# Issuing the first of two stores from ScalarE's queue instead of SyncE's in a row-normalising kernel

## The chip, the cores and the metric

The kernel runs on one core of one Trainium2 chip. The metric is the device time of one execution in microseconds (us), as the median of several runs; lower is better. The profile's span, from first to last instruction, is some 1.8 us shorter than the time of the same execution.

## The reference

Each of 1024 rows of 4096 floats is divided by its Euclidean norm.

```python
x = np.random.randn(1024, 4096).astype(np.float32)      # eps = 1e-12
norm = np.sqrt(np.sum(x ** 2, axis=-1, keepdims=True) + eps)
out = (x / norm).astype(np.float32)
```

## The kernel before

The rows lie in two groups. A group is one tile of 128 partitions with 4 rows each (8.39 MB), loaded by one transfer and stored by one. Both loads are issued at the start by SyncE. Per group, VectorE squares and sums row 3, ScalarE rows 0 to 2, and VectorE scales the rows. Only row 2 of the first group is scaled by both engines, ScalarE taking 7/8 of it.

```python
    for i in range(n_tiles):                       # n_tiles = 2
        g = RowGroups(...)
        load = nc.sync.dma_start(out=g.flat(), in_=x_t[i])
        if i == 0:
            first_load_to_front(nc, load.ins)      # ahead of the start-up barrier
        groups.append(g)

    for i, g in enumerate(groups):
        g.square_dve(R - 1)
        g.square_act(0)
        # ... cut: norm and scale of rows 0, 1 and 3 ...
        g.square_act(2)
        g.norm(2)
        if i < n_tiles - 1:
            g.scale_by_both(2)                     # ScalarE 3584 columns, VectorE 512
        else:
            g.scale(2)                             # VectorE alone
        store = nc.sync.dma_start(out=out_t[i], in_=g.flat())
    gpsimd_waits_for_last_store(nc, store.ins)     # shortens the end; not touched
```

## Time and profile before

| What | Value |
|---|---|
| Time, median of 6 runs | 81.93 us (81.73 to 81.96) |
| Span of the profiled run (82.04 us, 0.1 above the six) | 80.2 us |
| First store issued / second store issued | 38.99 / 56.76 us |
| Second load landed | 41.37 us |
| Last landing | 80.03 us |

The prediction shows the views that bound the kernel. Below, an *engine* without a name is one of the 16 DMA engines, and the *ring* of a queue is its part on one such engine. Each engine moves a transfer as eight data packets of 65,536 bytes and a last packet of 4 bytes, the *completion*; the transfer has landed when all 16 completions have arrived. In a table of windows, each line gives the window, its width, the busy times of the engines, the clock, the share of the 16 DMA engines, and GB/s. A data packet is booked whole in the window in which it starts. So when a window holds exactly one data packet of each engine, *share times width* is the mean time of that packet, and GB/s times width is 16 x 65,536 bytes = 1.05 MB. These are the first packets of the first store in the kernel before:

```profile
40.26:41.06 0.80, 0.00 (x0) 0.00 (x0) 0.00 (x0) 1.00 3.05 1311
41.06:42.88 1.82, 1.48 (x1) 1.48 (x1) 0.00 (x0) 1.00 0.00 0
42.88:43.48 0.60, 0.60 (x1) 0.60 (x1) 0.00 (x0) 1.00 4.03 1748
```

1311 GB/s x 0.80 us = 1.05 MB, so this is one packet of each engine, and 3.05 x 0.80 = 2.44 us is its mean time. The second packets (4.03 x 0.60 = 2.42 us) start from 42.88 on.

### The profile page before, as it was taken

The page shows a single profiled execution, that of the slowest core. Times are in us where ns is not written, and L with a number is a line of the kernel's source. Part 1 is how long each engine was busy: PE and PEld are TensorE (multiplying, and loading weights), DVE is VectorE, ACT ScalarE, POOL GpSimd, SP SyncE. Part 2 cuts the span into 40 slices and gives each one's busy share as a digit, 9 for nine tenths or more (in the row PEclk, how much of TensorE's full clock was granted, in tenths as well). Part 3 has the DMA queues.
Part 4 walks back from the last instruction along what each step waited for, and adds up shares of the span by engine and source line. Part 5 has one row for each costly group of instructions (what it writes and reads, how often), then busy time and mean ns, then how long its engine had stood idle before and what let it go on. Part 6 is the DMA issues. An engine that isn't in the chain of part 4 may idle for free.

```text
span 80.2 us, 93 instructions
## 1 busy us (share of the span) xinstructions
DVE 26.7 (33%) x21; ACT 29.7 (37%) x23; POOL 0.2 (0%) x4
## 2 busy tenths in 40 slices
DVE  0000000000099599960039995999200000000000
ACT  6000000000099999989439999950000000000000
POOL 0000000000000000000000000000000000000000
DMA  9099996699996699996699990999991999992990
GB/s 490 33 523 523 523 490 294 261 523 523 523 490 261 294 523 523 523 490 261 294 523 523 523 490 33 523 523 523 523 458 65 523 523 523 523 425 98 523 523 0
DMA packets 576, 33.55 MB, mean 418 GB/s; under 512 B 64, under 2 KB 64, under 8 KB 64
## 3 DMA queue, kind: packets, MB, share of 16 engines
q1 hardware_dynamic: 576, 33.55, 97.4%
HBM read 16.78 MB, written 16.78 MB: 418 GB/s over the span
## 4 chain that ended last, share of the span: by engine, by line
DMA 51%; ACT 10%; DVE 9%; issue 0%
DMA xt<-in_x_dram 51%; ACT sq_act L33 9%; DVE xt L64 9%; ACT rstd L53 1%; DVE rstd L59 0%
## 5 line engine op out<-in xcount | busy, mean ns | idle before, releaser
L33 ACT ACTIVATE sq_act<-xt 128x4096 f32<-128x4096 f32 x6 | 21.7, 3609 | 22.4 <-DMA xt<-in_x_dram 22.4
L42 DVE SCALAR_TENSOR_TENSOR sq_dve<-xt 128x4096 f32<-128x4096 f32 x2 | 8.9, 4426 | 26.4 <-DMA xt<-in_x_dram 26.4
L64 DVE TENSOR_SCALAR xt<-xt,rstd 128x4096 f32<-128x4096 f32 x7 | 16.5, 2353 | 0.2
L72 ACT ACTIVATE xt<-xt,rstd 128x3584 f32<-128x3584 f32 x1 | 3.3, 3283 | 0.2 <-DVE rstd L59 0.2
L53 ACT ACTIVATE rstd<-ssq,eps_t 128x1 f32<-128x1 f32 x8 | 2.1, 290 | 0.1
L59 DVE RECIPROCAL rstd<-rstd 128x1 f32<-128x1 f32 x8 | 1.3, 160 | 2.5 <-ACT rstd L53 2.5
L33 ACT ACT_TABLE_LOAD x1 | 1.3, 1283 | 0.8 <-PEq L258 0.8
L53 ACT ACT_TABLE_LOAD x1 | 1.3, 1283 | 0.0
L33 ACT ACTIVATION_READ_ACCUMULATOR sq_act<-xt 128x1 f32 x6 | 1.1, 187 | 0.0
L78 DVE TENSOR_SCALAR xt<-xt,rstd 128x512 f32<-128x512 f32 x1 | 0.5, 487 | 0.0
L211 DVE MEMSET eps_t<- 128x1 f32 x1 | 0.1, 59 | 0.9 <-PEq L258 0.9
L42 DVE DVE_READ_ACCUMULATOR sq_dve<-xt 128x1 f32 x2 | 0.2, 83 | 0.0
L258 POOL MEMSET const-uint8-127<- 128x1 uint8 x1 | 0.1, 103 | 0.0
L258 POOL MEMSET const-bfloat16-1.0<- 128x1 bf16 x1 | 0.1, 102 | 0.0
L258 POOL MEMSET const-float32-0.0<- 128x1 f32 x1 | 0.1, 99 | 0.2 <-issue 0.2
L258 POOL MEMSET const-float32-1.0<- 128x1 f32 x1 | 0.1, 99 | 0.0
## 6 DMA issues: line engine op xcount, KB each, us to landing
xt<-in_x_dram SPq DMA_DIRECT2D x2, 31.3
out_dram<-xt SPq DMA_DIRECT2D x2, 22.5
```

Of the source, the lines that this page charges most:

```text
L33: self.nc.scalar.activation(out=sq_a, in_=self.x[:, r], func=ACT_F.Square, accum_out=self.ssq[:, r : r + 1],)
L42: self.nc.vector.scalar_tensor_tensor(out=sq_v, in0=self.x[:, r], scalar=1.0, in1=self.x[:, r], op0=ALU.mult, op1=ALU.mult, accum_out=self ...
L53: self.nc.scalar.activation(out=self.rstd[:, r : r + n], in_=self.ssq[:, r : r + n], func=ACT_F.Sqrt, bias=self.eps_t,)
L59: self.nc.vector.reciprocal(out=self.rstd[:, r : r + n], in_=self.rstd[:, r : r + n])
L64: self.nc.vector.tensor_scalar_mul(out=self.x[:, r], in0=self.x[:, r], scalar1=self.rstd[:, r : r + 1])
L72: self.nc.scalar.activation(out=self.x[:, r, :cut], in_=self.x[:, r, :cut], func=ACT_F.Copy, scale=rstd,)
L78: self.nc.vector.tensor_scalar_mul(out=self.x[:, r, cut:], in0=self.x[:, r, cut:], scalar1=rstd)
L211: nc.vector.memset(eps_t, eps)
L258: nc = _bacc.Bacc("TRN2", target_bir_lowering=False, num_devices=1)
```

## The change

The first store moves to ScalarE's queue, behind the shared scale that ScalarE computes itself. SyncE then need not wait for another engine's result before this store, and the store does not lie in the same queue as the load before it.

```diff
-        store = nc.sync.dma_start(out=out_t[i], in_=g.flat())
+        queue = nc.scalar if i < n_tiles - 1 else nc.sync
+        store = queue.dma_start(out=out_t[i], in_=g.flat())
```

The scheduler also reorders ScalarE's instructions in the second group: the square root of row 3 comes first there, as in the first group.

## The prediction

> **What bounds the kernel now.** I read the page first, then the chain that ended last, then the waits of the DMA-issuing engine, then the timeline and the packet starts around the one moment that the change touches. The page's queue part comes first, because it says at once what can be won:
>
> ```profile
> span 80.2 us, 93 instructions
> DVE 26.7 (33%) x21; ACT 29.7 (37%) x23; POOL 0.2 (0%) x4
> q1 hardware_dynamic: 576, 33.55, 97.4%
> HBM read 16.78 MB, written 16.78 MB: 418 GB/s over the span
> ```
>
> No engine is busy for even half of the span, while the packets of the single queue fill 97.4% of what 16 DMA engines have: 78.1 of 80.2 us. The 16.78 MB in and 16.78 MB out are compulsory. The packet records show how they move: each engine carries 32 packets of 65,536 bytes, nearly all of 2.418 us, one straight after another, so 16 x 65,536 / 2.418 us = 434 GB/s while they flow, and 32 x 2.418 = 77.4 us is a floor under the span. The other 2.8 us are the 1.0 to 2.1 us before the first packets start and some 0.3 us between the last packet and its landing, with a few tenths in between. So the kernel is bound by the transfers, and no order of issue can win more than tenths.
>
> The chain of waits shows two places where compute stands between the transfers:
>
> ```profile
> 0.79 40.58 DMA xt<-in_x_dram
> 41.40 3.72 ACT sq_act L33 x2
> 54.38 2.35 DVE xt L64
> ```
>
> The second load lands at about 41.4; the second group's compute then runs to 56.73, and only then can the second store be issued. That chain ends long before the span does, because the second store then lies in the queue behind the first. The waits of the DMA-issuing engine and the timeline give the moments:
>
> ```profile
> SPq L240 <- DVE xt L64: 15.3, 1, 15.3
> SPq L240 <- ACT xt L72: 2.8, 1, 2.8
> ...
> 35.68 3.28 ACT L72 ACTIVATE xt<-xt,rstd 128x3584 f32<-128x3584 f32 x1 [0.23 <-DVE rstd L59]
> 38.99 18.11 SPq L240 DMA_DIRECT2D out_dram<-xt  x2
> 41.40 3.62 ACT L33 ACTIVATE sq_act<-xt 128x4096 f32<-128x4096 f32 x1 [2.43 <-DMA xt<-in_x_dram]
> ```
>
> The shared scale on ScalarE ends at 38.97, the first store is issued at 38.99, with no delay that the change could take away. ScalarE then idles for 2.43 us for the second load. What the engines do there, by the starts of their packets:
>
> ```profile
> 37.80:38.70 0.90, 0.00 (x0) 0.90 (x1) 0.00 (x0) 1.00 2.70 1165
> 38.70:40.26 1.56, 0.00 (x0) 0.27 (x1) 0.00 (x0) 1.00 0.00 0
> 40.26:40.47 0.21, 0.00 (x0) 0.00 (x0) 0.00 (x0) 1.00 0.01 0
> 40.47:41.06 0.59, 0.00 (x0) 0.00 (x0) 0.00 (x0) 1.00 4.13 1777
> ```
>
> The last load packets start by 38.7. Then nothing starts until 40.26, where the first of the load's 4-byte completion packets are (share 0.01, 0 GB/s). From 40.47 to 41.06 the store's first 16 packets start (1777 GB/s x 0.59 us = 1.05 MB). Packet by packet, the load's last data packets end between 40.265 and 41.053 on the 16 engines, a completion packet follows each at once, and on eleven engines a store packet 5 to 6 ns after that. On the other five the load ended at 40.27 to 40.49 and the store started only at 40.49 to 40.68. Those five tell the latency of the store: 1.50 to 1.69 us from issue to its first packets.
>
> **What the Trainium skill says.** "DMA: Bandwidth & Descriptors", section "Issuing engines are not separate DMA queues": transfers from ScalarE and SyncE run on the same 16 DMA engines and interleave; a second issuer saves only the issue time. The trace agrees as far as it can: the 434 GB/s above is the "Fabric ceiling" of 435 GB/s that the same page's "Specifications" give, so a second queue has no bandwidth to find. The same page, "Queues, rings and completion order": SP and ACT each have a ring of their own on each of the 16 engines, and an engine takes turns between its rings "at *packet* granularity"; the completion increment lands only after every earlier write of that engine, across its queues. The trace of before has one queue in this stretch, so it shows neither; it shows the opposite order, where the load's completion always goes ahead of the store's data.
>
> **The change part by part.** Removed: SyncE's issue of the first store (348 ns on an engine that then waits anyway): 0. Added: the same issue on ScalarE, some 0.35 us out of the 2.43 us for which it waits: 0. Its conditions are the same last instructions (the shared scale on both engines), so the issue stays at about 39.0.
>
> Moved by the scheduler: the order listing shows ScalarE's instructions of the second group in another order. The square root of the row that VectorE squared now goes first and waits for it; the order becomes that of the first group. Cost, counted from the landing: before, the last scale ends at 54.38 + 2.35 - 41.40 = 15.33 us. After, the first root starts when VectorE's accumulator is read, 45.75 + 0.08 - 41.40 + 0.04 = 4.47 us; in the first group the last scale starts 35.68 - 27.11 = 8.57 us after the first root, and takes 2.35: 15.39 us. So ScalarE's later second square (about 0.9 us) is paid back by VectorE having a second row to scale meanwhile, and the net is about +0.05 us, off the path.
>
> What matters is the ring. With its own ring the store does not have to queue behind the load's completion packet. Its descriptors reach the engines at about 38.99 + 1.5 to 1.7 = 40.5 to 40.7; five engines are then still in the load's last data packet (their ends: 40.73, 40.79, 40.87, 41.05, with one at 40.69 close by). If the engine takes turns, it serves a 65,536-byte store packet before the load's 4 bytes, and the completion comes 2.42 us later on that engine. One engine suffices, since all 16 must report. Then: second load seen at 41.40 + 2.42 = 43.82; compute ends at 43.82 + 15.39 = 59.21; second store issued at 59.23, its first packets at 60.7 to 60.9. The first store's data ends at the same time as before, 59.8 to 60.4, as the work is the same. So each engine idles some 0.4 to 0.9 us; on the one that ends last, 60.9 + 8 x 2.42 + 0.34 for the landing = 80.6 against 80.0 now. Sum: +0.6, with the five small gaps of before perhaps gone, say +0.5. Slack of 60.4 - 56.76 - 1.7 = 1.9 us in the second store swallows the rest of the 2.4.
>
> **The rivals.**
> First, nothing happens: the completion is already committed behind its data packet, or the ScalarE ring takes longer than 2.06 us to bring its first packets, and the load lands at 41.4 as before. For it: completion packets start 4 ns before the recorded end of the data packet; the first load of all took 1.0 to 2.1 us to its first packets. Against it: five observed latencies of 1.50 to 1.69. Time: 81.9.
> Second, the delay above: 82.4 to 82.5.
> Third, more than one store packet goes ahead of the completion, as if an engine stayed on a ring for several packets. Each further packet adds its 2.42 us fully, as the slack is gone: two make 84.8 to 85. Nothing in this trace speaks for it, and nothing excludes it.
> Fourth, a gain: the two queues close the five gaps of about 0.2 us. The engine that ended last had no gap, so at most 0.1: 81.8.
>
> **Range and chances.** No delay 0.32, one packet 0.58, several packets 0.08, gain 0.02. The prediction is 82.3, between the first two; 81.75 to 82.95 holds both with the spread of the runs (81.86 to 81.96) and 0.4 us for a slower ring. The 2% borders are 80.3 and 83.56. Faster would break the floor of the transfers: 0.01. Slower needs the third rival or a ScalarE ring much slower to start at the second load's cost: 0.09. Within 2%: 0.90.
>
> **What would show it.** In the changed profile: a second queue with half of the written bytes; the issue on ScalarE at 39.0; the second group's first square at 43.8 (one packet), 41.4 (nothing) or 46.2 (two); the second store issued 15.4 us after that; a stretch near 60.5 with no packet starting if the delay is there, and the first store landing at about its old 60.7 if the second store comes late, or about 2 us later if it comes in time and shares the engines. The step is wrong if the load is late by anything that isn't a multiple of 2.4 us, if the compute takes more than 15.6 us, or if packets get longer than 2.42 us where both queues are active: then sharing itself costs, which I count as nothing.

## The result and the profile after

The changed kernel takes 82.66 us (median of 6 runs, 82.54 to 82.77). Ratios here are the mean time of one kernel's fast runs over that of the other's in the same rounds, so not quite the ratio of the medians; this one is 1.0093 (95% interval 1.0079 to 1.0107), or +0.76 us. It is slower beyond the noise, within 2%, inside the predicted range, and clearly more than the predicted +0.4 us.

The page of the changed kernel, its span, queues and issues:

```profile
span 80.7 us, 93 instructions
q1 hardware_dynamic: 432, 25.17, 72.8%
q10 hardware_dynamic: 144, 8.39, 25.0%
out_dram<-xt ACTq DMA_DIRECT2D x1, 24.9
out_dram<-xt SPq DMA_DIRECT2D x1, 24.0
```

The bytes are the same, a quarter of them on a second queue, q10. The two shares sum to 97.8% of 80.7 = 78.9 us, against 78.1 before: the packets themselves became longer in sum, by 0.8 us per engine. The time is not an idle gap; it is inside packets. The timeline of the changed kernel around the store:

```profile
38.71 0.37 ACTq L241 DMA_DIRECT2D out_dram<-xt  x1
41.12 3.62 ACT L33 ACTIVATE sq_act<-xt 128x4096 f32<-128x4096 f32 x1 [2.44 <-DMA xt<-in_x_dram]
56.53 0.35 SPq L241 DMA_DIRECT2D out_dram<-xt  x1
```

The store is issued at 38.71 and the second load is seen at 41.12, 0.28 us earlier than before in both cases, because the first load happened to start earlier in this run. The load is *not* late. Measured from the load's landing, the compute ends after 56.51 - 41.12 = 15.39 us, as forecast, and the second store is issued in good time. What changed is in the packet starts of the changed kernel:

```profile
40.26:40.78 0.52, 0.00 (x0) 0.00 (x0) 0.00 (x0) 1.00 6.26 2017
40.78:43.54 2.76, 2.42 (x1) 2.42 (x1) 0.00 (x0) 1.00 0.00 0
43.54:43.88 0.34, 0.34 (x1) 0.34 (x1) 0.00 (x0) 1.00 7.11 3084
```

All 16 first packets of the store start by 40.78, each some 6 ns after the load's completion packet on its engine, so the five gaps of before are gone. But they take 6.26 x 0.52 = 3.26 us on average instead of 2.44; one by one, 3.05 to 3.47 us. The second packets start only from 43.54, and from there all run at 2.418 us. Measured from the landing of the second load to the last landing, the kernel before needs 80.03 - 41.37 = 38.66 us and the changed one 80.53 - 41.10 = 39.43: +0.77 us, the whole difference. I call this lengthening of the first packets the *stall*.

At the end of the first store, the turn-taking that the prediction expected does show. The same view of the changed kernel where the second store, back on SyncE's queue, meets the first:

```profile
58.03:58.36 0.33, 0.00 (x0) 0.00 (x0) 0.00 (x0) 1.00 7.33 3178
60.44:60.78 0.34, 0.00 (x0) 0.00 (x0) 0.00 (x0) 1.00 7.11 3084
62.86:63.20 0.34, 0.00 (x0) 0.00 (x0) 0.00 (x0) 1.00 7.14 3084
```

The first line holds the first store's last data packets, the second line the *second* store's first ones (7.11 x 0.34 = 2.42 us: no stall). By the packet records, the first store's completion packets come at 60.45 on one engine and at 62.92 to 63.18 on the other 15, behind a packet of the second store. So a completion can be overtaken by another queue's data, but this one was overtaken by a store issued 4 us ahead, and the load's by a store issued 1.6 to 2.1 us ahead was not.

### The profile page after: what moved, and what is told of

It is laid out like the page before. It is cut to its first block, busy times and chain, and to the rows that moved or that the text cites. A ratio compares the mean times of both kernels' runs of the same rounds, so it can differ in the third digit from the quotient of the medians.

```text
span 80.7 us, 93 instructions
## 1 busy us (share of the span) xinstructions
DVE 26.8 (33%) x21; ACT 29.8 (37%) x23; POOL 0.2 (0%) x4
## 4 chain that ended last, share of the span: by engine, by line
DMA 50%; ACT 10%; DVE 9%; issue 0%
DMA xt<-in_x_dram 50%; ACT sq_act L33 9%; DVE sq_dve L42 6%; DVE xt L64 3%; ACT rstd L53 1%; DVE rstd L59 0%
```

## The experiments

Fourteen kernels ran, 13 with correct results and one wrong. Each diff is against the changed kernel unless it says otherwise. I use *lead* for the time from a transfer's issue to the moment at which an engine ends the data of the transfer before it, and *extra* for how much a packet exceeds 2.418 us. Single-engine figures come from the packet records. The first theories were: A, a ring's first transfer is slow; B, ScalarE's path is slow; C, every change of ring is.

### 1. Is it the ring's first use?

```diff
+    warm = scratch_pool.tile([P, 16], F32)
+    nc.scalar.dma_start(out=warm, in_=x_t[0][:, :16])
```

> The changed kernel, with one small load (128x16 floats, 8 KB) put on ScalarE's queue at the very start, so that its ring has been used long before the first store. Theory A (a ring's first transfer takes about 0.9 us longer from issue to data, whichever engine issues it): the store's first packets take 2.42 to 2.47 us again instead of 3.05 to 3.47; if its data is then ready 1.5 to 1.7 us after the issue, the late engines serve a store packet ahead of the load's completion and the second load lands 2.4 us later, time 82.3 to 82.5; otherwise 81.9. Theory B (ScalarE's path is always that slow): first packets 3.05 to 3.47 us as in the changed kernel, time 82.6 to 82.7. Theory C (an engine that changes from one busy ring to another stalls once): the same as B.

Measured: 82.70 us, ratio 1.0095 (1.0080 to 1.0110). The first packets of the store with the warmed ring, and the small load's line among the issues:

```profile
40.47:40.92 0.45, 0.00 (x0) 0.00 (x0) 0.00 (x0) 1.00 7.09 2330
```

```profile
warm<-in_x_dram ACTq DMA_DIRECT2D x1, 8.0 KB, 23.6
```

7.09 x 0.45 = 3.19 us: the stall is unchanged on 15 engines (extra 0.63 to 1.06 us). The sixteenth had ended the load 0.24 us before the store reached it and showed an extra of only 0.04 us. Theory A falls. The 8 KB load brings a surprise: it took 23.6 us to land. Each engine got eight pieces of 64 bytes and moved one of them after each 65,536-byte load packet, every 2.42 us from 6.5 us on. So turns are taken packet by packet, as the prediction assumed.

### 2. Is it ScalarE?

The loads go to ScalarE's queue and both stores to SyncE's. Ordering edges without waits keep each engine's order as in the changed kernel, and the helper that moves the first load to the front now looks on ScalarE; neither is shown.

```diff
-        load = nc.sync.dma_start(out=g.flat(), in_=x_t[i])
+        load = nc.scalar.dma_start(out=g.flat(), in_=x_t[i])
...
-        queue = nc.scalar if i < n_tiles - 1 else nc.sync
+        queue = nc.sync
```

> The rings exchanged: both loads are issued by ScalarE, both stores by SyncE, the instructions of each engine otherwise in the order of the changed kernel. Theory A (a ring's first transfer is slow): SyncE's ring is now the unused one, so the first store's first packets take 3.0 to 3.5 us and the time is 82.5 to 82.8. Theory B (ScalarE's path is slow): the store starts as in the kernel before, first packets 2.42 to 2.47 us, time 81.9, or 82.4 if the store overtakes the load's completion. Theory C (change of ring): as A.

Measured: 82.84 us, ratio 1.0114 (1.0101 to 1.0127), just above the 82.5 to 82.8 of theories A and C. The store's first packets:

```profile
40.22:41.14 0.92, 0.00 (x0) 0.00 (x0) 0.00 (x0) 1.00 3.38 1140
```

3.38 x 0.92 = 3.11 us. The stall appears on SyncE's ring as well: 13 engines had an extra of 0.64 to 1.05 us, and three had 2.45 to 2.46 us packets. Those three fit engines that had been idle when the store arrived. B falls. A new theory, D, suggested itself: the stall is paid when work from another ring reaches an engine that is still moving data, and not when it reaches an idle one.

### 3. A second store on the other ring, and an earlier first store

The second store alone on ScalarE's queue, where it is issued 3 us before the engines get free:

```diff
-        queue = nc.scalar if i < n_tiles - 1 else nc.sync
+        queue = nc.sync if i < n_tiles - 1 else nc.scalar
```

> The first store stays on SyncE's queue as in the kernel before; the second store is issued on ScalarE's queue, which has not been used until then. It is issued at about 56.8, some 3 us before the engines finish the first store. If the slow first transfer is a latency that runs from the issue (2.4 to 2.7 us), it is hidden: 81.9, first packets 2.42 us. If it is a stall of the first packet itself whenever that packet is served, or a stall of the change of ring: first packets of 3.0 us or more, time 82.5 to 82.8.

Measured: 81.91 us (81.78 to 82.41), ratio 1.0013 (0.9991 to 1.0035), the same as before. The second store's first packets:

```profile
59.69:60.29 0.60, 0.00 (x0) 0.00 (x0) 0.00 (x0) 1.00 4.13 1748
```

4.13 x 0.60 = 2.48 us: one engine had an extra of 0.77 us, the other 15 none, at leads of 3.0 to 3.6 us. The profiled run was one of the slower of six (82.22 us), so the number of engines hit may differ from run to run. A change of ring can be free on most engines, and C in its plain form falls too.

The first store 0.8 us earlier on ScalarE's queue, by letting VectorE scale row 2 alone:

```diff
-        if i < n_tiles - 1:
+        if False:
             g.scale_by_both(2)
```

> The changed kernel, with the last row of the first group scaled by VectorE alone (2.35 us in place of 3.28), so that the store is issued 0.93 us earlier. If the cost of the changed kernel is a latency from the issue, most of its 0.65 to 1.05 us per engine is hidden: first packets 2.4 to 2.6 us. But the store's descriptors then reach the engines while the load's last data packet runs, so an engine that takes turns serves a store packet ahead of the load's completion: the second load lands at about 43.5 to 43.9 instead of 41.1, and the second store is issued near 59. Time 81.9 to 82.4. If the stall belongs to the first packet or to the ring whatever the lead: packets still over 3 us, time 82.6 or more.

Measured: 82.75 us, ratio 1.0114 (1.0098 to 1.0130). The load's last packets, then the store's first ones:

```profile
37.73:38.99 1.26, 0.18 (x1) 0.00 (x0) 0.00 (x0) 1.00 2.04 832
40.36:41.42 1.06, 0.00 (x0) 0.00 (x0) 0.00 (x0) 1.00 3.06 989
```

The store's first packets still took 3.06 x 1.06 = 3.24 us, although issued earlier: all 16 engines had an extra, 0.37 to 1.10 us, at leads of 2.4 to 3.5 us. The load was not overtaken either, against my expectation: it landed at 41.67, not at 43.5. It was late by some tenths because its last packets took 2.04 x 1.26 = 2.57 us.

### 4. A later store, and controls on SyncE's queue

Theory D made an odd forecast: on ScalarE's queue a *later* store should be cheaper. ScalarE scales the whole of row 2 here:

```diff
-        cut = 7 * self.D // 8
+        cut = self.D
```

The part of `scale_by_both` for VectorE is taken out with it.

> The changed kernel, but ScalarE scales the whole row alone (about 3.75 us in place of 3.28), so the store is issued about 0.47 us LATER on ScalarE's queue, near 39.2, and reaches the engines near 40.7, when most of them have finished the load (40.3 to 40.8). Theory D (a store from another ring that reaches an engine which is still moving the load costs a stall of 0.6 to 1.1 us after the load's end; one that reaches an idle engine starts at once): most first packets take 2.42 to 2.47 us after an idle gap of 0.1 to 0.5 us, and the later store makes the kernel FASTER than the changed one: 81.9 to 82.3. Theory B or C (every first packet after a change of ring is slow, or ScalarE's path is): first packets again over 3 us, time 82.7 to 83.1.

Measured: 82.38 us (82.15 to 82.68), ratio 1.0060 (1.0041 to 1.0080). That is faster than the changed kernel's 1.0093, though the two intervals just touch, and 0.08 us above the expected range. The store's packets:

```profile
40.51:41.04 0.53, 0.00 (x0) 0.00 (x0) 0.00 (x0) 1.00 4.73 1979
```

4.73 x 0.53 = 2.51 us. Fifteen engines had nothing to do, or were just done, when the store came, and had an extra of 0.03 to 0.05 us. The one that was still in the load's last packet (lead 1.63 us) had 0.78 us. So D holds packet by packet. The gain in time is weaker: the profiled run is the slowest of the six, and with one engine stalled it took 39.46 us from the load's landing to the last landing, as long as the changed kernel. The control has the same late store on SyncE's queue:

> The control to the run before: the same late issue, but on SyncE's queue. Gaps of 0.1 to 0.5 us on the engines that ended the load early, first packets 2.42 to 2.47 us, 81.9 to 82.2 by every theory. The difference between the two is what the ring costs at this moment of issue: about 0 by theory D, 0.7 by B or C.

Measured: 82.11 us, ratio 1.0036 (1.0022 to 1.0049). All first packets were 2.42 to 2.47 us after gaps of up to 0.7 us on the engines that ended early. The ring's price at this moment of issue is thus about 0.2 us instead of 0.76, though the two intervals overlap.

The pair shows one thing more. On engines that were idle, the store's first packets came 1.3 to 1.8 us after the issue in both runs. So ScalarE's ring is not slower to bring a store, which is the second half of the prediction's first rival.

The control to the earlier store, also on SyncE's queue:

> The control to the run with the earlier issue: the last row of the first group scaled by VectorE alone, the store on SyncE's queue, issued near 37.9. By every theory the store waits in the same ring behind the load: no gap, first packets 2.42 us, 81.7 to 81.9; it would be the best kernel of the study by up to 0.1 us. If the load's last packets are longer than 2.45 us here too, the lengthening seen with the earlier issue is the issue's and not the second ring's.

Measured: 82.30 us, ratio 1.0057 (1.0045 to 1.0070). This missed my expectation of 81.7 to 81.9. The load's last packets, then the store's first:

```profile
37.75:38.40 0.65, 0.03 (x1) 0.00 (x0) 0.00 (x0) 1.00 4.32 1613
40.67:41.32 0.65, 0.00 (x0) 0.00 (x0) 0.00 (x0) 1.00 3.73 1613
```

No stall (3.73 x 0.65 = 2.42 us), but the load's last packets took 4.32 x 0.65 = 2.81 us, 0.21 to 0.59 us too long on every engine. So a store that is issued 2.9 to 3.5 us ahead slows the load in front of it even in the same ring. It is a second effect, and not the changed kernel's: there the load's last packets took 2.418 to 2.428 us. Its mechanism stays open.

### 5. Can the load's completion be overtaken at all?

Row 2 of the first group is left unscaled here, so the result is wrong and the store can go at 34.85.

```diff
-            g.scale_by_both(2)
+            pass
```

> A wrong result on purpose: the third row of the first group is not scaled, so the store can be issued on ScalarE's queue near 34.7, and its descriptors reach the engines near 36.2, before the load's last data packet starts (37.8 to 38.3). If an engine chooses what comes next one packet ahead, the store's first packet now goes ahead of the load's completion: the second load lands near 43.5 to 43.9, 2.4 us late. If it takes turns without looking ahead, one store packet also goes ahead of the last data packet, and the load lands 4.8 us late, near 46. If a load is never overtaken by a store of another ring, it lands at 41.1 to 41.4. The second store is issued about 14 to 15 us after the landing; time 82 to 83 for one packet, 84 to 85 for two.

Measured: 83.2 us in three fast runs, ratio 1.0165 (1.0150 to 1.0181), 0.2 us above what was expected for one packet. The profiled run counts as slow (85.0 us), so I rely only on the order of its packets. The load's last data packets (15 of 16), then 15 store packets with the load's last packet on the sixteenth engine, then 15 completions of the load with the next store packets:

```profile
37.98:38.55 0.57, 0.00 (x0) 0.00 (x0) 0.00 (x0) 1.00 5.97 1725
41.50:42.20 0.70, 0.00 (x0) 0.00 (x0) 0.00 (x0) 1.00 3.45 1498
44.00:44.60 0.60, 0.00 (x0) 0.00 (x0) 0.00 (x0) 1.00 4.04 1748
```

On 15 engines exactly one store packet went between the load's last data packet and its completion, which came at 44.02 to 44.55. On the sixteenth, one store packet went ahead of the load's last data packet and a second ahead of the completion (46.42), so the load landed at 46.77 instead of 44.91. That delay could by itself make this run the slow one; no fast run was profiled to show it. The last load packets of the 15 took 3.3 to 3.8 us here. So the prediction's mechanism exists. But it needs a longer lead. Over all runs (the leads of 3.6 to 4.3 us are those of second stores in fast runs), no completion was overtaken at leads of 1.5 to 3.6 us, both cases occurred between 3.6 and 4.0, and at 4.0 us and more all were overtaken. A lead of 4.0 us is one packet (2.42 us) plus the 1.5 to 1.7 us that a store needs to reach the engine, so it seems that the store has to be there before the last data packet *starts*. The 8 KB load of experiment 1 agrees: it was issued at 0.78 us, the first packets of the large load ended 3.3 to 3.8 us after that, and yet all 16 engines moved the large load's second packet before the first piece of the small one.

### 6. Which turns cost, and how much lead frees them?

Load to load. Dummy work on ScalarE, writing into the tile, holds the second load back until the first is nearly done, and from there on all transfers are ScalarE's. Ordering edges as in experiment 2.

```diff
+        if i == 1:
+            for r, n in enumerate((D, D, D, D, 2816)):
+                nc.scalar.activation(out=g.x[:, r % R, :n],
+                    in_=eps_t.to_broadcast([P, n]), func=ACT_F.Square)
-        load = nc.sync.dma_start(out=g.flat(), in_=x_t[i])
+        load = (nc.sync if i == 0 else nc.scalar).dma_start(out=g.flat(), in_=x_t[i])
...
-        queue = nc.scalar if i < n_tiles - 1 else nc.sync
+        queue = nc.scalar
```

> Two loads on two rings: the second load is issued on ScalarE's queue, held back by dummy work on ScalarE until about 1.5 to 2.5 us before the first load's data ends (so that it reaches the engines during the first load's last packets); both stores follow on ScalarE's queue, so the only change of ring with work in flight is from load to load. If the stall belongs to any packet of another ring that arrives beside work in flight: the second load's first packets take 3.0 to 3.5 us, time 82.6 to 82.9. If it belongs to the turn from a load to a store: first packets 2.42 us there, and 81.8 to 82.1.

Measured: 82.18 us, ratio 1.0036 (1.0015 to 1.0057). The second load's first packets:

```profile
20.85:21.42 0.57, 0.00 (x0) 0.00 (x0) 0.00 (x0) 1.00 4.70 1840
```

4.70 x 0.57 = 2.68 us: an extra of 0.254 us on each of the 16 engines alike, at leads of 2.2 to 2.75 us. Neither expectation fits; a turn from load to load costs, but less. The store behind it in the same ring had no extra at leads of 1.8 to 2.3 us. The control:

> The control: the same late second load, all four transfers on SyncE's queue. No stall at the change of load, first packets 2.42 us, time 81.8 to 82.1 by every theory; if the held-back load comes too late, both this and the run before show the same idle gap.

Measured: 82.26 us, ratio 1.0039 (1.0027 to 1.0052), above the expected 81.8 to 82.1. No extra over 0.015 us at the turn from load to load. It is no clean control in time: its first store came out at 39.47 us, 0.8 us later than in the other kernel, and pays the gaps of a late store. The two times cannot be set against each other; the packets can.

Store to store, with the changed kernel's lead. A pass that multiplies part of row 2 by 1 holds the second store back:

```diff
+            nc.vector.tensor_scalar_mul(
+                out=g.x[:, 2, :2816], in0=g.x[:, 2, :2816], scalar1=1.0)
-        queue = nc.scalar if i < n_tiles - 1 else nc.sync
+        queue = nc.sync if i < n_tiles - 1 else nc.scalar
```

> Two stores on two rings: the first on SyncE's queue, the second on ScalarE's, held back by a dummy pass on VectorE of about 1.6 us until about 1.4 to 2.0 us before the first store's data ends, the same lead that the changed kernel's first store has. If the stall belongs to any change of ring with so short a lead: the second store's first packets take 3.0 to 3.5 us, time 82.6 to 82.9. If it belongs to the turn from load to store: 2.42 us, 81.8 to 82.0.

Measured: 82.67 us, ratio 1.0092 (1.0076 to 1.0108), the loss of the changed kernel reproduced with no load in sight. The control keeps both stores on SyncE's queue:

> The control: the same held-back second store on SyncE's queue. First packets of 2.42 us, with small idle gaps on the engines that end early; 81.8 to 82.1 by every theory.

Measured: 81.84 us, ratio 0.9984 (0.9970 to 0.9997). The second store's first packets, on ScalarE's queue and then on SyncE's:

```profile
59.61:60.07 0.46, 0.00 (x0) 0.00 (x0) 0.00 (x0) 1.00 7.13 2280
```

```profile
59.69:60.22 0.53, 0.00 (x0) 0.00 (x0) 0.00 (x0) 1.00 4.58 1979
```

7.13 x 0.46 = 3.28 us against 4.58 x 0.53 = 2.43 us, with the queue as the only difference in the code. At leads of 1.4 to 1.9 us all 16 engines stalled by 0.67 to 1.10 us on the other ring, and none on the same. The stall needs neither ScalarE's compute, nor a load, nor the reordering.

Finally the lead alone, from store to store on two rings, with 1850 and 900 columns in the dummy pass instead of 2816:

> The two stores on two rings again, the second issued about 0.5 us earlier than in the run that stalled, so its lead over the first store's end is about 2.0 to 2.4 us. If the stall is the remainder of a longer start-up that runs from the issue (about 2.6 us on a ring that is not the busy one, against 1.5 on the same ring or an idle engine): extra of the first packets 0.2 to 0.6 us, time 82.2 to 82.4. If it is a fixed price of the turn: 0.7 to 1.1 us again, 82.6 to 82.8.

> The same with a lead of about 2.5 to 2.9 us. Start-up from the issue: extra 0 to 0.15 us, time 81.9 to 82.0. Fixed price of the turn that only vanishes when the descriptors are there before the last data packet starts (lead over about 3.9 us): 0.7 to 1.1 us, 82.6 to 82.8; but the earlier run with a lead of 3.0 to 3.6 us showed it on one engine of 16 only.

Measured: 82.66 us, ratio 1.0086 (1.0072 to 1.0099), and 82.67 us, ratio 1.0094 (1.0080 to 1.0108). The second store's first packets in the two:

```profile
59.50:60.10 0.60, 0.00 (x0) 0.00 (x0) 0.00 (x0) 1.00 5.43 1748
```

```profile
59.50:60.20 0.70, 0.00 (x0) 0.00 (x0) 0.00 (x0) 1.00 4.66 1498
```

5.43 x 0.60 = 3.26 us and 4.66 x 0.70 = 3.26 us, as with the short lead. So it is a fixed price, not the rest of a start-up that runs from the issue. The results for a store that joins a store, by lead:

| Lead, store after store, two rings | Extra of the first packets | Kernel |
|---|---|---|
| 1.5 to 1.9 us | 0.67 to 1.10 us, 16 of 16 engines | held back by 2816 columns |
| 2.0 to 2.4 us | 0.66 to 1.04 us, 16 of 16 | 1850 columns |
| 2.4 to 2.9 us | 0.66 to 1.06 us, 16 of 16 | 900 columns |
| 3.0 to 3.6 us | 0.77 us on one, 0 on 15 | not held back (experiment 3) |
| 3.9 to 4.2 us | 0, and the completion is overtaken on 15 of 16 | the changed kernel's second store |

No version beats the kernel before by anything to speak of; the held-back second store on SyncE's queue is at 0.9984, with an interval that barely excludes 1.

## Why the prediction was right or wrong

- **Bound by the transfers; gain at most tenths.** Right: same bytes, and the loss of 0.77 us shows in the packets' sum (0.8 us per engine).
- **The issue itself costs nothing, the reordering about 0.05 us off the path.** Right: ScalarE's idle time of 2.43 us swallowed the 0.37 us, and the compute took 15.39 us against 15.33.
- **"Its descriptors reach the engines at about 38.99 + 1.5 to 1.7", and then "it serves a 65,536-byte store packet before the load's 4 bytes".** The second half is the step that failed. The load's completion came first on all 16 engines, and the load landed at 41.10. Turns are taken, but the choice seems to be made about one packet ahead. The run with the store at 34.85 and the changed kernel's second store show overtaking; leads up to 3.6 us do not. The lead here was 1.6 to 2.1 us. The arrival does not seem to be at fault: leads of 2.4 to 3.6 us are longer than the 1.3 to 1.8 us of a store to idle engines, and there too the completion went first. The look-ahead itself is an inference from these leads.
- **The first rival, no delay of the load, at 81.9 us.** The event was right, its price was wrong. I gave this case no cost, and the prediction said so at its end: "then sharing itself costs, which I count as nothing". That term measured 0.63 to 1.05 us per engine, 0.83 us on average by the packet records. The small gaps of before, on five engines, come off it; between the two landings +0.77 us remains.
- **The sum.** The delay case gave +0.5 to +0.6 us, and 82.3 was set between it and a free case. (With the third rival's 0.08 the prediction's own chances average to 82.46.) The measured 82.66 lies in the range by luck, for another reason than the one most of the weight was on; the forecast of +0.4 us fell short of the measured +0.76.
- **The third and fourth rivals**, several packets ahead and a gain, did not occur in the changed kernel. Two packets ahead were seen on one engine of the run with the store at 34.85.

One line of the kernel before was passed over. The prediction lists the packets as "nearly all of 2.418 us", with "a few tenths in between" in the span. Most of these tenths are one long packet per engine, the first of the first load:

```profile
1.00:2.20 1.20, 0.00 (x0) 1.07 (x1) 0.00 (x0) 1.00 2.56 874
```

2.56 x 1.20 = 3.07 us, an extra of 0.65 us on average, on engines that were idle. So the trace already showed that a first packet can be longer than 2.42 us. No run tests whether this has the same cause as the stall.

Why a packet from another ring stalls is not settled. Shown is when. A store pays it when it joins an engine within its last packet of the other ring, with a lead of 1.5 to 2.9 us. The price is about the same whichever of the two rings joins. It is absent in the same ring, for a store on an idle engine, and for a store that joins a store with 3.0 us and more (but for one engine). For a store that joins a *load* with a lead of 2.4 to 3.5 us, the extra is there on all 16 engines, the second effect mixes in, and the two were not separated further. A load that joined a load paid 0.25 us.

## What to carry to other kernels

Where the packets fill the DMA engines, as here (97.4% of the span), ask of a second issuing queue how its transfer will join the one in front; none of these runs gained by it. Here a large store that followed in the same ring in good time joined without a gap. The same store from another ring cost about 0.8 us, unless it was issued at least 3 us before the end of the store in front or found the engines idle. In the profile, look for this not in idle gaps but in the duration of the first packets after the turn, and compare kernels from one landing to the next, so that the scatter of the first load drops out.

## What the Trainium skill lacked or had wrong

- "DMA: Bandwidth & Descriptors", section "Issuing engines are not separate DMA queues": it says that several issuers only save issue time. It lacks the price: 0.63 to 1.10 us on the first 65,536-byte packet when a store from another ring joins busy engines with a lead of 1.5 to 2.9 us (82.67 against 81.84 us with nothing but the queue changed).
- The same page, "Queues, rings and completion order": turns at packet granularity agree with the runs (an 8 KB load in eight pieces per engine needed 23.6 us beside a stream of 65,536-byte packets). It lacks when a turn is decided: a completion packet was overtaken on 15 of 16 engines at leads of 3.9 to 4.2 us, and on none at 1.6 to 2.1 us.
- The same page, "Latency and other measured facts": it gives about 0.6 us to the first byte and does not say from where it counts. From the end of the issuing instruction (0.38 us) the earliest packet of the first load in the kernel before agrees, 1.015 - 0.383 = 0.63 us, while the last engine's first packet came at 2.12. Stores took longer: their first packets on idle engines came 1.3 to 1.8 us after the start of an issue of 0.35 to 0.37 us, on either queue.
- No page has it that a store issued 2.9 to 3.5 us before the end of a load in the same ring lengthens that load's last packets by 0.21 to 0.59 us (82.30 us against 81.82 for the kernel before).
